# Two conditioning vectors of layer 1 computed on VectorE in layer 0's feed-forward, instead of on TensorE in layer 1's mixer

## The chip, the cores and the metric

The kernel runs on one core of a Trainium2 chip. The metric is device time in microseconds (us) of one execution. Five engines matter here, each with its own queue of instructions that it works off in order: PE (TensorE: matrix products; PEld is its weight load), DVE (VectorE), ACT (ScalarE), POOL (GpSimd, nearly unused) and SP (SyncE, which issues nearly all DMA transfers). An instruction that waits for a semaphore holds back all that stands behind it on its engine.

## The reference

Two blocks of two layers each, on 256 tokens of width 1024, all in float32. The change lies in the first block, whose layers are conditioned by a vector `c`:

```python
c_act = jax.nn.silu(c)
for l in range(DEPTH):                       # DEPTH = 2
    ada = c_act @ w_ada[l] + b_ada[l]        # 1024 x 6144
    sh1, sc1, gt1, sh2, sc2, gt2 = split(ada, 6)
    u = x * (1.0 + sc1) + sh1
    y = mixer(u, ...)                        # projections, attention, 31-tap convolution, gates
    x = layer_norm(DN_ALPHA * x + (1.0 + gt1) * y, ...)
    u = x * (1.0 + sc2) + sh2
    h = square(relu(u @ w_up[l])) @ w_down[l]   # width 4096
    x = layer_norm(DN_ALPHA * x + (1.0 + gt2) * h, ...)
```

Inside the mixer the convolution's output goes through a layer norm over 512 channels (`conformer_conv`) and a SiLU. The second block (three attention branches, gated feed-forward, RMS norms) follows and ends in an RMS norm that is the output, 256x1024.

The six vectors of a layer are numbered 0 to 5 in the order sh1, sc1, gt1, sh2, sc2, gt2; (1, 3) is sh2 of layer 1, (1, 4) is sc2 of layer 1.

## The kernel before, in words

**Weights.** Every weight matrix is cut into pieces of 128x2048 elements (1 MB). `fetch` loads one into `raw` (3 buffers, SP, L133) and splits it into a high part `whi` (ACT CAST, two halves, L139) and the rest `wlo` (DVE subtraction, two halves, L140), 4 buffers each. PE multiplies high by high, high by low and low by high: `ws2` (L176 with `whi`, then L178 with `wlo`) for the feed-forward's up-projection, `as_` (L207, L208, L209, with L208 on `wlo`) for its down-projection, `ws` (L161, L162, L165) elsewhere. So no weight is used before DMA, ACT and DVE are done with it.

**Feed-forward (`ffn1`).** Sixteen pieces of up-weight and sixteen of down-weight, here called u0 to u15 and d0 to d15. A round for column block c does up-weight uc, then the down-weight of three blocks before, d(c-3). Between them ACT squares and DVE splits the activations (L152 writes the low part `s`); the `s4` pool has 7 buffers, so L152 of block c can't write before PE has read the last of the high part of block c-3: it waits for the end of the down-weight d(c-3) on PE. The last three down-weights d13, d14, d15 are held back for the handover, where they are multiplied part by part of the output (`out.tail`). Of these three the first, d13 (`third` in `fetch`), has its high and low part not in `whi` and `wlo` but in the pool `ada`, which has 2 buffers.

**Conditioning.** There are two ways to compute the six vectors.
- On DVE (`ada_work`): per 128x1024 piece one DMA of 512 KB (L397) into the pool `ada`, and one multiply-and-sum instruction (L386, with a short readout behind it) for a vector kept by columns, or L408 and L410 for a gate. Eight pieces make a vector. The load of the next piece is issued before the multiply of the one at hand; with 2 buffers a load waits until the multiply two pieces before is done.
- On PE (`ada_pe`): per quarter of a vector two DMAs of 512 KB (L445), a block of small products (L451, 16 matmul records in the trace), an ACT copy (L454), and products with a column of ones (L461, 4 records, with the sum on DVE in L464) or, for gates, `ada_gate` (L430, L431, L433).

**Side work.** `track` gives a generator a rate, `tick` (called by PE's code with the time of what it has just issued) advances it, `finish` runs out what is left. In layer 0's feed-forward `ada_work` runs 24 pieces (gt2 of layer 0, then sc1 and sh1 of layer 1) with 30 steps per 160 us of ticks; in the mixer of layer 1 `ada_pe` runs three vectors, 12 quarters, with 25 steps per 80 us.

**Order.** PE's order is that of the code. DVE, ACT and SP are ordered by a scheduler when the program is built, except in the handover between two layers (`handover`), which is written out by hand: last parts of the down-projection, gates (L778), residual (L782), statistics (L785 on), normalisation (L795), transposes (L749), and the first products of the next layer.

The functions touched follow, with the profile's line numbers.

Of the kernel before, what the change touches and what calls it, by code (L numbers as in the profile page):

```python
# [12 lines left out]
AF = mybir.ActivationFunctionType  # L13
ALU = mybir.AluOpType
# [46 lines left out]
PARTS = ((0, 512), (512, 768), (768, 1024))  # L61
ADA_PE = [(0, 4), (0, 3), (0, 2), (1, 3), (1, 4), (1, 2)]


class Net:
# [609 lines left out]
    def handover(self, out, ch, nxt=None):  # L675
# [4 lines left out]
        with self.tc.manual_schedule(engines={E.PE, E.DVE, E.Activation}):  # L680
# [3 lines left out]
            fill = ch.front(1)  # L684
# [3 lines left out]
            if ch.ln_rms:  # L688
                out.tail(1, PARTS[2])
            ch.stats(0, itertools.islice(fill, 2))  # L690
            ch.transposed(0, 8 if ch.ln_rms else 0)
# [144 lines left out]
    class RMSNorm(Norm):  # L836
# [66 lines left out]
        def finish(self, h, fill=()):  # L903
            nc, net, u = self.nc, self.net, self.u
            fill = iter(fill)
            if not u:
                y, o = self.y[h], net.out[h * P:(h + 1) * P, :]
                nc.scalar.mul(y[:, :512], y[:, :512], self.rs[h])
                nc.sync.dma_start(o[:, :512], y[:, :512])
                if h:  # L910
                    i = nc.vector.scalar_tensor_tensor(y[:, 512:], net.x[:, h, 512:], self.rs[h], self.g[:, 512:],
                                                       op0=ALU.mult, op1=ALU.mult)
                else:
                    i = nc.vector.tensor_scalar(y[:, 512:], y[:, 512:], self.rs[h], None, op0=ALU.mult)
                nc.sync.dma_start(o[:, 512:], y[:, 512:])
                yield
                yield [i]
                return
# [4 lines left out]
            for k in range(4):  # L923
                i = nc.scalar.copy(hi[k], ps[k])
# [48 lines left out]
    def conv_ln(self, l, cv, hc):  # L973

        nc = self.nc
# [5 lines left out]
        for h in range(2):  # L981
# [6 lines left out]
            z = self.ev()  # L988
            nc.vector.tensor_scalar(z, p, mu, rs, op0=ALU.subtract, op1=ALU.mult)
            zs.append(z)  # L990
# [19 lines left out]
    def mixer1(self, l, u, ps):  # L1010
# [21 lines left out]
        if first:  # L1032
            for ct in range(2):
                self.glu(ps[6 + ct], ct, hp)
            for g in range(3):
                keep(g, ps[2 * g:2 * g + 2] and enumerate(ps[2 * g:2 * g + 2]))
            ada = self.track(self.ada_pe(ADA_PE[:3]), 25, 56)
            conv = self.track(convs[0], 31, 40)
# [5 lines left out]
        else:  # L1044
            keep(2, ps)
            ada = self.track(self.ada_pe(ADA_PE[3:]), 25, 80)
            for ct in range(4):
# [86 lines left out]
    def ffn1(self, l, u, ps):  # L1134
        nc = self.nc
        segs = [(0, 5), (1, 1), (1, 0)] if l == 0 else [(1, 5)]
        ada = self.track(self.ada_work(segs), 8 * len(segs) + 6, 160 if l == 0 else 80)
# [553 lines left out]
```

## Time and profile before

| | |
|---|---|
| median of 3 runs | 1702.15 us (1702.01 to 1704.94) |
| profiled execution | 1700.27 us, of which the trace's span is 1698.5 us |
| mean granted TensorE clock | 0.998 |
| bytes moved by DMA | 347.38 MB, mean 205 GB/s |

The span divides into: start (0 to 65 us), mixer of layer 0 (65 to 195), handover (195 to 222), feed-forward of layer 0 (222 to 395, the last rounds of it from 300), handover (395 to 425, with the last down-weights already from 377), mixer of layer 1 (425 to 570), handover, feed-forward of layer 1 (600 to 770), second block (770 to the end).

In the rows below, times on the left are microseconds from the span's start. In a timeline a row is a run of alike instructions on one engine: start, busy time, engine, line, operation, what is written and read, count, and in brackets how long the engine had been idle before and what released it. A table by windows gives per stretch its length, the busy time of each engine with the number of instructions, the granted clock (1.00 is full), the DMA engines' busy share and GB/s.

### The profile page before, as it was taken

Reading aid. Unit: us, or ns where it says so; the run is one execution under the profiler, and the core shown is the slowest. Engines: PE = TensorE matmul, PEld = TensorE weight load, DVE = VectorE, ACT = ScalarE, POOL = GpSimd, SP = SyncE. Lnnn points to the kernel's source line nnn. Section 1 sums busy time; section 2 is a strip of 40 time slices with the busy share of each in tenths; the row PEclk is TensorE's granted clock in tenths of the full one; section 3 lists DMA queues with packets and bytes.
Section 4 is the critical chain, followed back from the end, with each engine's and each line's share of the span. In section 5 each row is a group of like instructions: output and inputs, shape, how many; then the busy total and the mean of one; then the engine's idle time right before and its main releaser. Section 6 shows DMA issues by size and latency. Waiting matters only on the chain.

```text
span 1698.5 us, 25989 instructions
## 1 busy us (share of the span) xinstructions
PE 1658.0 (98%) x10090; PEld 1437.4 (85%) x10090; DVE 1271.2 (75%) x2485; ACT 955.9 (56%) x1750; POOL 2.6 (0%) x12
## 2 busy tenths in 40 slices
PE   6999999999999999999999999999999999999998
PEld 5888888888888888887988898888889888988887
DVE  7999798588997796568665777766675567877665
ACT  3565375475355475544567755555465687455553
POOL 0000000000000000000000000000000000000000
PEclk9999999999999999999999999999999999999999
DMA  8886468495865386645634443655454444445551
GB/s 343 349 312 232 167 230 340 170 345 209 305 251 201 111 295 216 220 154 194 227 130 152 150 163 138 242 191 198 152 209 170 152 149 149 174 163 209 195 181 46
DMA packets 59975, 347.38 MB, mean 205 GB/s; under 512 B 6558, under 2 KB 10700, under 8 KB 25676
## 3 DMA queue, kind: packets, MB, share of 16 engines
q1 hardware_dynamic: 59852, 345.73, 55.8%
q8 instruction: 79, 1.29, 0.3%
q14 instruction: 44, 0.36, 0.1%
HBM read 344.63 MB, written 2.64 MB: 204 GB/s over the span
## 4 chain that ended last, share of the span: by engine, by line
PE 92%; DVE 5%; ACT 1%; DMA 1%; issue 1%; SPq 0%; DVEq 0%; ACTq 0%
PE ps L176 23%; PE ps L178 12%; PE ps L208 8%; PE ps L209 8%; PE ps L207 8%; PE ps L161 5%; PE ps L162 4%; PE ps L165 4%; PE ps L223 3%; PE ps L229 3%; PE ps L224 3%; PE ps L339 1%; PE ps L451 1%; PE ps L499 1%; PE ps L476 1%; DVE wlo L140 1%
## 5 line engine op out<-in xcount | busy, mean ns | idle before, releaser
L140 DVE TENSOR_TENSOR wlo<-raw,whi 128x1024 fp32r<-128x1024 f32 (+1 forms) x526 | 622.3, 1211 | 242.2 <-ACT whi L139 241.6
L139 ACT CAST whi<-raw 128x1024 fp32r<-128x1024 f32 (+1 forms) x526 | 527.4, 1043 | 266.0 <-PE ps L209 62.3
L176 PE MATMUL ps<-ub,whi 128*128 128x512 f32 x1088 | 273.2, 393 | 0.0
L176 PEld LDWEIGHTS ps<-ub,whi 128*128 128x128 f32 x1088 | 198.6, 188 | 37.5
L207 PE MATMUL ps<-whi,s 128*128 128x512 f32 (+1 forms) x448 | 168.3, 376 | 0.0
L208 PE MATMUL ps<-wlo,s 128*128 128x512 f32 (+1 forms) x448 | 168.1, 375 | 0.0
L209 PE MATMUL ps<-whi,s 128*128 128x512 f32 (+1 forms) x448 | 167.7, 374 | 0.0
L176 PE MATMUL ps<-ua,whi 128*128 128x512 f32 x640 | 165.7, 401 | 0.0
L178 PEld LDWEIGHTS ps<-ub,wlo 128*128 128x128 f32 x1088 | 148.3, 190 | 12.3 <-DVE wlo L140 1.8
L178 PE MATMUL ps<-ub,wlo 128*128 128x256 f32 x1088 | 151.8, 282 | 1.3 <-DVE wlo L140 1.3
L176 PEld LDWEIGHTS ps<-ua,whi 128*128 128x128 f32 x640 | 115.3, 188 | 27.8 <-issue 5.7
L209 PEld LDWEIGHTS ps<-whi,s 128*128 128x128 f32 x448 | 84.3, 188 | 15.9 <-DVE s L152 0.7
L207 PEld LDWEIGHTS ps<-whi,s 128*128 128x128 f32 x448 | 84.5, 189 | 14.5 <-issue 0.6
L189 ACT COPY ev<-ps 128x256 f32<-128x256 f32 x136 | 50.3, 370 | 82.6 <-PE ps L178 82.5
L969 DVE SCALAR_TENSOR_TENSOR s<-s,dw,s 128x255 f32<-128x255 f32 (+14 forms) x240 | 96.7, 461 | 0.0
L208 PEld LDWEIGHTS ps<-wlo,s 128*128 128x128 f32 x448 | 84.5, 189 | 13.6
L178 PEld LDWEIGHTS ps<-ua,wlo 128*128 128x128 f32 x640 | 87.2, 190 | 6.5
L161 PE MATMUL ps<-ua,whi 128*128 128x256 f32 x352 | 89.3, 292 | 0.2 <-DVE s L958 0.2
L178 PE MATMUL ps<-ua,wlo 128*128 128x256 f32 x640 | 89.0, 282 | 0.0
L162 PE MATMUL ps<-ua,whi 128*128 128x256 f32 x352 | 85.9, 282 | 0.0
L161 PE MATMUL ps<-s,whi 128*128 128x256 f32 x320 | 81.9, 288 | 1.3 <-ACT s L151 1.3
L162 PE MATMUL ps<-s,whi 128*128 128x256 f32 x320 | 81.3, 286 | 1.2 <-DVE s L152 1.2
(301 smaller groups left out, 2828.5 us busy)
## 6 DMA issues: line engine op xcount, KB each, us to landing
raw<-in_w_fgu_dram SPq DMA_DIRECT2D x44, 1024.0 KB, 4.8
raw<-in_w_up_dram SPq DMA_DIRECT2D x32, 1024.0 KB, 5.1
raw<-in_w_down_dram SPq DMA_DIRECT2D x32, 1024.0 KB, 5.4
raw<-in_w_in_dram SPq DMA_DIRECT2D x32, 1024.0 KB, 4.8
ada<-in_w_ada_p_dram SPq DMA_DIRECT2D x48, 512.0 KB, 4.4
raw<-in_w_gate_dram SPq DMA_DIRECT2D x24, 1024.0 KB, 4.8
raw<-in_w_fd_dram SPq DMA_DIRECT2D x22, 1024.0 KB, 4.8
raw<-in_w_in_b_dram SPq DMA_DIRECT2D x18, 1024.0 KB, 6.5
```

Source lines behind the costliest of these rows:

```text
L139: nc.scalar.copy(hi[:, a:b], raw[:, a:b])
L140: nc.vector.tensor_sub(lo[:, a:b], raw[:, a:b], hi[:, a:b].bitcast(F32))
L161: mm(ps, whi[:, b], ahi[:, k, :], start=j == 0, stop=False)
L162: mm(ps, whi[:, b], alo[:, k, :], start=False, stop=False)
L165: mm(ps, wlo[:, b], ahi[:, k, :], start=False, stop=j == n - 1)
L176: mm(p2, whi[:, (blk + k) * P:(blk + k + 1) * P], both[:, :, k, :], start=k == 0, stop=False)
L178: mm(p[:, :S], wlo[:, (blk + k) * P:(blk + k + 1) * P], uhi[:, k, :], start=False, stop=k == KT - 1)
L207: mm(ps, ahi[:, k, tok], whi[:, cols], start=first, stop=False, **grp)
L208: mm(ps, ahi[:, k, tok], wlo[:, cols], start=False, stop=False, **grp)
L209: mm(ps, alo[:, k, tok], whi[:, cols], start=False, stop=last, **grp)
L223: mm(p, ahi[:, k, tok], whi[:, cols], start=k == 0, stop=False)
L969: nc.vector.scalar_tensor_tensor(cv[:, ct, d:], hp[:, ct, :S - d], wk, cv[:, ct, d:], op0=ALU.mult, op1=ALU.add)
```

## The change

`ADA_PE` loses (1, 3) and (1, 4): they are computed by `ada_work` in layer 0's feed-forward, which now has 40 pieces instead of 24, with 46 steps per 160 us of ticks instead of 30. The mixer of layer 1 keeps one vector on PE, 4 quarters. Three smaller edits: the convolution's layer norm forms its normalised values on ACT instead of DVE; layer 0's mixer spreads its PE conditioning over 46 us of ticks instead of 56; and the last handover's output is scaled and stored in quarters for the second half of the tokens.

```diff
-ADA_PE = [(0, 4), (0, 3), (0, 2), (1, 3), (1, 4), (1, 2)]
+ADA_PE = [(0, 4), (0, 3), (0, 2), (1, 2)]
@@ handover
-            ch.stats(0, itertools.islice(fill, 2))
+            ch.stats(0, itertools.islice(fill, 2 if ch.u else 3))
@@ RMSNorm.finish, the output
-                nc.scalar.mul(y[:, :512], y[:, :512], self.rs[h])
-                nc.sync.dma_start(o[:, :512], y[:, :512])
+                step = 256 if h else 512
+                for a in range(0, 512, step):
+                    s, r = slice(a, a + step), slice(512 + a, 512 + a + step)
+                    nc.scalar.mul(y[:, s], y[:, s], self.rs[h])
+                    nc.sync.dma_start(o[:, s], y[:, s])
...
@@ conv_ln
-            nc.vector.tensor_scalar(z, p, mu, rs, op0=ALU.subtract, op1=ALU.mult)
+            nm = self.small(1, "nmu")
+            nc.vector.tensor_scalar(nm, mu, -1.0, rs, op0=ALU.mult, op1=ALU.mult)
+            nc.scalar.activation(z, p, AF.Identity, bias=nm, scale=rs)
@@ mixer1, layer 0, then layer 1
-            ada = self.track(self.ada_pe(ADA_PE[:3]), 25, 56)
+            ada = self.track(self.ada_pe(ADA_PE[:3]), 25, 46)
-            ada = self.track(self.ada_pe(ADA_PE[3:]), 25, 80)
+            ada = self.track(self.ada_pe(ADA_PE[3:]), 9, 60)
@@ ffn1
-        segs = [(0, 5), (1, 1), (1, 0)] if l == 0 else [(1, 5)]
+        segs = [(0, 5), (1, 3), (1, 4), (1, 1), (1, 0)] if l == 0 else [(1, 5)]
```

The scheduler puts DVE's and SP's instructions of layer 0's feed-forward in another order. Three places follow. Names end in numbers that count buffers; they differ between the two programs.

**First place: DVE, the L152 from which on conditioning multiplies stand between the weights again, after two rounds without.** Before, this is L152 of block 11 (`s_516`), which waits for the end of d8 on PE; behind it come u12 (`wlo_3270`) and, with one multiply between, d9 (`wlo_3331`).

```order
L152 TENSOR_TENSOR s_516_3325<-ev_3275,s_515_3324 128x512
L431 TENSOR_TENSOR G_495_3193<-ps_3360,b_445_2882 128x256
L433 TENSOR_SCALAR G_495_3193<-G_495_3193 128x256
L386 ISA ada_3264,ada_513_3299<-ada_3264,c_row_92,par_95 128x1024
L386 ISA ada_513_3299 128x1
L140 TENSOR_TENSOR wlo_3270<-raw_3267,whi_3269 128x1024 x2
```

Now it is L152 of block 10 (`s_514`), which waits for the end of d7; behind it come u11 (`wlo_3216`) and then d8 (`wlo_3272`).

```order
L152 TENSOR_TENSOR s_514_3266<-ev_3221,s_513_3265 128x512
L386 ISA ada_3116,ada_478_3039<-ada_3116,c_row_92,par_4_101 128x1024
L386 ISA ada_478_3039 128x1
L386 ISA ada_3145,ada_478_3039<-ada_3145,c_row_92,par_4_101 128x1024
L386 ISA ada_478_3039 128x1
L140 TENSOR_TENSOR wlo_3216<-raw_3213,whi_3215 128x1024
L386 ISA ada_3207,ada_478_3039<-ada_3207,c_row_92,par_4_101 128x1024
L386 ISA ada_478_3039 128x1
L140 TENSOR_TENSOR wlo_3216<-raw_3213,whi_3215 128x1024
L386 ISA ada_3210,ada_478_3039<-ada_3210,c_row_92,par_4_101 128x1024
```

The place lies one round earlier. From it to the end of the feed-forward 21 pieces of conditioning are left on DVE, where before 8 were, and three of them stand ahead of the second half of the first weight behind it, where before there was one.

**Second place: SP, the loads around the first place.** Before, a load of a conditioning piece and a load of a weight alternate; `ada_3364` is the first that waits for a multiply behind L152 of block 11, and `raw_3328` (d9) is ahead of it.

```order
L397 DMA ada_3264<-in_w_ada_t_dram 128x1024
L133 DMA raw_3267<-in_w_up_dram 128x2048
L397 DMA ada_3297<-in_w_ada_t_dram 128x1024
L133 DMA raw_3328<-in_w_down_dram 128x2048
L397 DMA ada_3364<-in_w_ada_t_dram 128x1024
L133 DMA raw_3367<-in_w_up_dram 128x2048
```

Now two conditioning loads stand between two weights; `ada_3207` waits for the multiply of `ada_3116`, and `ada_3210` for that of `ada_3145`.

```order
L397 DMA ada_3116<-in_w_ada_t_dram 128x1024
L397 DMA ada_3145<-in_w_ada_t_dram 128x1024
L133 DMA raw_3213<-in_w_up_dram 128x2048
L397 DMA ada_3207<-in_w_ada_t_dram 128x1024
L397 DMA ada_3210<-in_w_ada_t_dram 128x1024
L133 DMA raw_3269<-in_w_down_dram 128x2048
```

Ahead of the load that waits there is now one weight (u11); d8 (`raw_3269`) stands behind two waiting loads. Before, two weights (u12 and d9) were ahead of it.

**Third place: DVE, the end of layer 0's feed-forward.** Before, the low parts of d13 (`ada_3641`), d14 (`wlo_3694`) and d15 (`wlo_3726`) stand ahead of L152 of block 15 (`s_567`), which waits for the end of d12 on PE; the first two weights of the next layer (`wlo_3734`, `wlo_3742`) stand ahead of L778.

```order
L140 TENSOR_TENSOR ada_3641<-raw_3638,ada_3640 128x1024 x2
L190 TENSOR_TENSOR ev_3646<-ps_3647,ev_3646 128x256
L140 TENSOR_TENSOR wlo_3694<-raw_3691,whi_3693 128x1024 x2
L190 TENSOR_TENSOR ev_3646<-ps_3666,ev_3646 128x256
L140 TENSOR_TENSOR wlo_3726<-raw_3723,whi_3725 128x1024 x2
L152 TENSOR_TENSOR s_567_3688<-ev_3646,s_566_3687 128x512
L140 TENSOR_TENSOR wlo_3734<-raw_3731,whi_3733 128x1024 x2
L140 TENSOR_TENSOR wlo_3742<-raw_3739,whi_3741 128x1024 x2
L778 TENSOR_TENSOR ev_3814<-ps_2560,G_495_3193 128x512
```

Now the low parts of d14 (`wlo_3748`), d13 (`ada_3695`) and d15 (`wlo_3780`) stand behind L152 of block 15 (`s_587`), with two multiplies among them.

```order
L152 TENSOR_TENSOR s_587_3742<-ev_3700,s_586_3741 128x512
L386 ISA ada_3685,ada_562_3586<-ada_3685,c_row_92,par_95 128x1024
L386 ISA ada_562_3586 128x1
L140 TENSOR_TENSOR wlo_3748<-raw_3745,whi_3747 128x1024
L386 ISA ada_3688,ada_562_3586<-ada_3688,c_row_92,par_95 128x1024
L386 ISA ada_562_3586 128x1
L140 TENSOR_TENSOR wlo_3748<-raw_3745,whi_3747 128x1024
L140 TENSOR_TENSOR ada_3695<-raw_3692,ada_3694 128x1024 x2
L140 TENSOR_TENSOR wlo_3780<-raw_3777,whi_3779 128x1024 x2
L767 TENSOR_TENSOR pl_b_3807<-pl_b_3807,ada_562_3586 128x8
L778 TENSOR_TENSOR ev_3868<-ps_2567,G_466_2992 128x512
L140 TENSOR_TENSOR wlo_3788<-raw_3785,whi_3787 128x1024 x2
```

The next layer's two weights (`wlo_3788`, and `wlo_3796` further on) have moved behind L778, one on each side of L782, ahead of the statistics L785. On ACT the casts of d13 (`ada_3694`, which waits for the multiply of `ada_3685`, since it takes that buffer) stand ahead of those of d14 (`whi_3747`).

## Rows read from the trace of the kernel before

**Rows 1.** The page: the chain that ended last, share of the span by engine

```profile
PE 92%; DVE 5%; ACT 1%; DMA 1%; issue 1%; SPq 0%; DVEq 0%; ACTq 0%
```

**Rows 2.** Windows: layer 1's mixer; busy time of PE, PEld, DVE, ACT, POOL

```profile
425.00:500.00 75.00, 75.00 (x597) 63.50 (x599) 71.56 (x166) 34.94 (x64) 0.00 (x0) 1.00 0.75 284
```

**Rows 3.** Window 417 to 486, PE and PEld, instructions of L451 alone

```profile
417.00:486.00 69.00, 8.56 (x128) 3.34 (x128) 1.00 0.83 309
```

**Rows 4.** The same window, instructions of L461 alone

```profile
417.00:486.00 69.00, 4.00 (x32) 4.52 (x32) 1.00 0.83 309
```

**Rows 5.** Timeline of DVE in layer 0's feed-forward, around L152 of block 11

```profile
331.18 0.69 DVE L152 TENSOR_TENSOR s<-ev,s 128x512 fp32r<-128x512 f32 x1 [4.47 <-PE ps L208]
...
332.45 1.28 DVE L386 CUSTOM_DVE_ANT_0 ada<-ada,c_row,par 128x1024 f32<-128x1024 f32 x1
...
333.65 2.35 DVE L140 TENSOR_TENSOR wlo<-raw,whi 128x1024 fp32r<-128x1024 f32 x2
```

**Rows 6.** Timeline of SP's DMA issues: the first one after 305.02

```profile
333.76 0.33 SPq L397 DMA_DIRECT2D ada<-in_w_ada_t_dram  x1
```

**Rows 7.** Windows of 5 us in the same stretch

```profile
325.00:330.00 5.00, 5.00 (x27) 4.25 (x26) 0.42 (x1) 3.56 (x6) 0.00 (x0) 1.00 0.00 0
335.00:340.00 5.00, 5.00 (x30) 4.42 (x31) 5.00 (x6) 0.97 (x3) 0.00 (x0) 1.00 1.00 382
```

**Rows 8.** Timeline of PE: u12 from 331.39, and the first of d9

```profile
331.39 2.19 PE L176 MATMUL ps<-ub,whi 128*128 128x512 f32 x8
334.93 1.21 PE L178 MATMUL ps<-ub,wlo 128*128 128x256 f32 x8 [1.34 <-DVE wlo L140]
...
338.77 0.40 PE L207 MATMUL ps<-whi,s 128*128 128x512 f32 x1
```

**Rows 9.** The page: the largest cast on ACT, and DMA issues with KB and us to landing

```profile
L139 ACT CAST whi<-raw 128x1024 fp32r<-128x1024 f32 (+1 forms) x526 | 527.4, 1043 | 266.0 <-PE ps L209 62.3
...
raw<-in_w_fgu_dram SPq DMA_DIRECT2D x44, 1024.0 KB, 4.8
...
raw<-in_w_in_b_dram SPq DMA_DIRECT2D x18, 1024.0 KB, 6.5
```

**Rows 10.** Timeline of DVE at the end of layer 0's feed-forward

```profile
368.10 2.35 DVE L140 TENSOR_TENSOR ada<-raw,ada 128x1024 fp32r<-128x1024 f32 x2
...
377.37 0.69 DVE L152 TENSOR_TENSOR s<-ev,s 128x512 fp32r<-128x512 f32 x1 [0.64 <-PE ps L208]
377.98 4.62 DVE L140 TENSOR_TENSOR wlo<-raw,whi 128x1024 fp32r<-128x1024 f32 x4
382.52 0.68 DVE L778 TENSOR_TENSOR ev<-ps,G 128x512 f32<-128x512 f32 x1
...
386.02 0.42 DVE L778 TENSOR_TENSOR ev<-ps,G 128x256 f32<-128x256 f32 x1 [1.30 <-PE ps L209]
...
390.57 0.54 DVE L795 TENSOR_SCALAR x<-x,mv,r_r 128x512 f32<-128x512 f32 x1
```

**Rows 11.** Timeline of PE there: d13 begins, its first part of the output ends, the transposes

```profile
377.34 0.40 PE L207 MATMUL ps<-ada,s 128*128 128x512 f32 x1
...
381.29 0.39 PE L209 MATMUL ps<-whi,s 128*128 128x512 f32 x1
...
391.40 1.03 PE L749 MATMUL ps<-con,x 128*128 128x128 f32 x8
```

**Rows 12.** Windows in layer 0's mixer

```profile
160.00:171.00 11.00, 7.87 (x62) 7.28 (x60) 10.88 (x20) 9.86 (x17) 0.00 (x0) 1.00 0.69 255
...
172.00:173.00 1.00, 1.00 (x4) 1.00 (x5) 1.00 (x2) 0.00 (x0) 0.00 (x0) 0.50 0.02 8
...
174.00:175.00 1.00, 1.00 (x7) 1.00 (x6) 1.00 (x2) 0.00 (x0) 0.00 (x0) 0.50 0.89 197
```

**Rows 13.** Timeline of DVE in layer 1's mixer: the convolution's layer norm

```profile
527.00 0.70 DVE L986 BATCH_NORM_STATS2 bn<-ps 128x6 f32<-128x512 f32 x1 [1.61 <-PE ps L984]
...
530.75 0.80 DVE L989 TENSOR_SCALAR ev<-ps,mv,r_r 128x512 f32<-128x512 f32 x1
```

More of the change, by code (lines that the diff above doesn't have):

```diff
@@ L907, in finish @@
                 y, o = self.y[h], net.out[h * P:(h + 1) * P, :]
-                nc.scalar.mul(y[:, :512], y[:, :512], self.rs[h])
-                nc.sync.dma_start(o[:, :512], y[:, :512])
[L910 to L915, printed above, removed]
+                step = 256 if h else 512
[3 more added lines that the diff above has]
+                    nc.sync.dma_start(o[:, s], y[:, s])
+                    if h:
+                        i = nc.vector.scalar_tensor_tensor(y[:, r], net.x[:, h, r], self.rs[h], self.g[:, r],
+                                                           op0=ALU.mult, op1=ALU.mult)
+                    else:
+                        i = nc.vector.tensor_scalar(y[:, r], y[:, r], self.rs[h], None, op0=ALU.mult)
+                    nc.sync.dma_start(o[:, r], y[:, r])
                 yield
```

## The prediction

> **What bounds the kernel now.** I read the chain of waits first: PE holds 92% of it, DVE 5% [rows 1]. So a microsecond less of PE work counts nearly in full wherever PE has no gap, and a microsecond of waiting on DVE counts where PE runs out of weights. Next the windows, because the change takes work from one stage and adds it to another. In layer 1's mixer PE is busy in all 75 us and DVE in 71.56 of them [rows 2]: PE bounds, DVE is close behind. In layer 0's feed-forward the timeline of DVE shows a hole: L152 of block 11 waits 4.47 us for PE, and only behind it come the conditioning multiplies again [rows 5]. SP, whose next conditioning load waits for such a multiply, issues nothing until 333.76 [rows 6], so the DMA engines move nothing at 325 to 330 and then run flat out, 382 GB/s at 335 to 340 [rows 7]. PE pays 1.34 us for it, at the low part of u12 [rows 8]. What the reader is to see: one DVE instruction that waits for the end of a product also stops the loads of the weights two products later.
>
> **What the change takes away.** Eight quarters go from PE in layer 1's mixer, each 16 records of L451 and 4 of L461. In the window 417 to 486 exactly eight ran: 128 records in 8.56 us and 32 in 4.00 [rows 3, 4], together 12.56 us. Records of neighbours overlap a little at their modelled ends, so I take 12.3 (11.5 to 12.56). PE has no gap there, so this is on the path as long as DVE keeps up. DVE loses almost nothing in that stage, and its idle time is 3.4 us of 75 [rows 2], and 1.6 before the convolution's statistics [rows 13]. PE comes to the convolution's transposes 12.3 us sooner; if DVE can only close these 5.0 us, 7.3 are lost again. The other end is no loss, since idle DVE time past 500 helps too and PE has other products to do between the transposes and the use of the normalised values. I take 1.5 lost, near the lower end.
>
> **What it adds: the hole.** Sixteen more multiplies of 1.20 us (start to next start, 332.45 to 333.65 [rows 5]) and sixteen more loads enter layer 0's feed-forward, and the order shows the hole one round earlier, with 21 multiplies left behind it, where 8 were, and one weight loaded ahead of the waiting load, not two. From T, the release of L152 of block 10: L152 0.69, two multiplies 2.40, half a subtraction 1.14 (four take 4.54, 377.98 to 382.52 [rows 10]) give the low part of u11 at T + 4.2. PE wants it 2.2 us after its start, as 1.34 before 334.93 [rows 8], so it stands some 1.9. Then d8: its load is behind a conditioning load that waits for the second multiply, so it is issued at about T + 3.5, with two 0.52 MB loads ahead, the first of them from T + 1.9. 2.1 MB at 382 GB/s take 5.5 us, and a 1 MB load needs 4.8 to land [rows 9], 2.05 more than its bytes; so it lands at T + 9.45. Cast of a half 1.04 [rows 9] and subtraction 1.14: T + 11.6. PE comes from u11 (7.38 with its 1.34 of waiting, so 6.04 [rows 8], and 1.9 here) at T + 8.1 to 9, so it stands 2.6 to 3.3. With half a microsecond on d8's second half that makes 5.2. It isn't won back: a round is 11.15 us (four rounds from 331.39 to 377.34 less 1.34 [rows 8, 11]), and half a round now needs two conditioning loads and a weight, 2.1 MB or 376 GB/s, as much as the queue gave. DVE has 19 multiplies and 20 halves before L152 of block 15, 45.5 us of the 55.8, without the rest of its work. So small waits may follow, up to 2.5. I take 6.5 less the 1.34 that goes: **+5.2** (from +0.5, if only u11 waits, to +6.4).
>
> The Trainium skill ("Perfetto Trace Analysis", Roofline) gives about 435 GB/s as the ceiling of one core's 16 DMA engines. By that 2.1 MB would take 4.8 us and d8 wait 0.7 less; the trace's 382 decides, and nothing above uses the page.
>
> **What it adds: the end of the feed-forward.** Here I am surest. Before, d13's low part is made at 368.10, nine microseconds before L152 of block 15 [rows 10], and PE goes from d12 into d13 without a gap at 377.34 [rows 11]. Now it stands behind that L152, which can't begin before d12 has ended. From E, the end of d12: L152 0.65; the multiply to 1.85, which alone frees the buffer for d13's high part; three casts on ACT at 1.04 (two halves of d13, one of d14) to 4.95; half of d14 on DVE to 6.1; the second multiply to 7.3; d14's second half to 8.4; d13's first half at 9.5. PE's second product of d13 wants it at 0.2, so PE stands **9.3 us**. Without the casts the DVE work alone is 6.4: that is the lower bound.
>
> The handover adds more. The next layer's two weights were subtracted before L778 (four halves from 377.98 [rows 10]); now they sit around L782. The first needs d13's raw buffer, free at E + 10.7: landing after 4.8 at 15.5, cast 16.5, two halves to 18.8; L782 to 19.5; the second weight lands 2.75 later and is done at 21.8; two statistics 0.75; and from the next L778 to L795 it was 4.55 (386.02 to 390.57 [rows 10]), so L795 stands at E + 27.1. Before it stood at 13.2 (377.37 to 390.57). PE's transposes L749 came right behind it [rows 11]. So **+13.9** up to there, PE's 9.3 included. With 6.5 for the load (the median of that weight [rows 9]) it is 15.6; the lower bound stays 6.4.
>
> **What it adds: the clock.** In layer 0's mixer PE was busy only 7.87 of 11 us and then the granted clock fell to 0.50, which is 1.2 instead of 2.4 GHz, in the windows from 172 to 175 [rows 12]: three microseconds that did the work of 1.5. Stands of 9.3 and some 4 us are longer than that. I take **+1.5** (0 to 3.0, for neither or both).
>
> The Trainium skill ("TensorE: Matmul & The Clock Gate", HAM oscillation) says that each long enough idle gap of PE is paid again with a cold start of the next products. By that it would be 3.0; in this trace one drop stands behind two short gaps and the long gap of before isn't there to tell, so I stay at one.
>
> **The small edits.** In layer 0's mixer two DVE instructions go to ACT (the like one takes 0.80 [rows 13]) while PE waits: of 3.1 us idle [rows 12] some may go, but ACT was busy 9.86 of 11 us too. I take -0.6 (-3.1, all of it, to +1.6, the two on ACT late). The output in quarters: no row shows such a store; one 128x512 DVE step of 0.68 [rows 10] is my bound on both sides, 0 my value.
>
> **The sum.** -12.3 + 1.5 + 5.2 + 13.9 + 1.5 - 0.6 = +9.2 us. On the profiled execution's 1700.27 that is 1709.5; the median of the runs is 1.9 higher, so 1711.4. The likeliest case's own range is 1705 to 1718. All low ends together give -9.5 (1692.7), all high ends +23.1 (1725).
>
> **Rivals.**
> - *The cover holds (faster).* The loads catch up, the hole costs 0.5, the end only the 6.4 of DVE's order, and PE's 12.3 shows. Point that decides: whether the two terms in layer 0 together stay below 8 us. 1702.15 + 0.5 + 6.4 - 12.3 - 0.6 = 1696. For it: before, a hole of 28 us in the loads cost only 1.34. Against: d13's place behind L152 doesn't depend on loads. With less at the end than its DVE order says, 1692. Chance 0.17.
> - *About even.* Hole 2, end 9.3, no drop of the clock, nothing given back in the mixer: 1702. Chance 0.08.
> - *The saving isn't one.* DVE sets the mixer's end: 7.3 of the 12.3 are lost there, the rest as forecast: 1702.15 + 9.2 + 5.8 = 1717. For it: DVE at 71.56 of 75 [rows 2]. Against: PE waits for it nowhere in those 75 us. Chance 0.15.
>
> That leaves 0.60 for the forecast. Faster by over 0.2% (3.4 us, about what a measurement here can tell from none) 0.17, within 0.08, slower 0.75. The range goes from 1697, which leaves out about one in ten below, to 1719.
>
> **What would show it.** Right: in the changed profile PE waits 8 to 10 us for the cast or the subtraction of an `ada` tile at the first products behind d12; L749 behind it waits for L795; two or three gaps of 1 to 3 us at L178 and L208 one round ahead of where the 1.34 was; L451 in layer 1's mixer down to four blocks and that stage 10 to 12 us shorter; a stretch at clock 0.50 behind the long gap. Wrong: d13 follows d12 without a gap, or the mixer of layer 1 is as long as before because L984 or the products behind it wait for DVE.

## The result, and the profile after

The changed kernel takes 1726.65 us (median of 5 runs, 1724.21 to 1729.98), the kernel before 1702.15 in the same comparison: ratio 1.0141, 95% interval [1.0126, 1.0155]. It is slower, as forecast, but by 24.5 us where 9.2 were forecast, and outside the stated range, which ended at 1719; even all the high ends of the forecast's terms together gave 1725, so a term was missing and not only mis-sized. The profiled execution has a span of 1724.8 us, 26.3 more than before.

The chain that ended last, of the page after, to be held beside [rows 1]:

```profile
PE 82%; DVE 10%; DMA 4%; ACT 2%; issue 1%; SPq 0%; ACTq 0%; DVEq 0%
```

PE has lost ten hundredths of the chain to DVE, DMA and ACT: it stands where it didn't. To see where, take one mark per stage. The transposes L749 of the second half of the tokens are the last act of each handover that waits. In the timeline of PE, of the kernel before (start, busy time, and in brackets the wait):

```profile
214.16 1.07 PE L749 MATMUL ps<-con,x 128*128 128x128 f32 x8 [1.27 <-DVE x L795]
401.17 1.06 PE L749 MATMUL ps<-con,x 128*128 128x128 f32 x8 [1.27 <-DVE x L795]
587.23 1.07 PE L749 MATMUL ps<-con,x 128*128 128x128 f32 x8 [1.28 <-DVE x L795]
```

and of the kernel after:

```profile
225.57 1.07 PE L749 MATMUL ps<-con,x 128*128 128x128 f32 x8 [1.23 <-DVE x L795]
439.20 1.07 PE L749 MATMUL ps<-con,x 128*128 128x128 f32 x8 [1.28 <-DVE x L795]
612.83 1.07 PE L749 MATMUL ps<-con,x 128*128 128x128 f32 x8 [1.28 <-DVE x L795]
```

The differences between neighbours are the stages' lengths; with the first L161 of layer 0's mixer as the first mark (63.34 before, 65.06 after) and the span's end as the last:

| us | start | layer 0's mixer | its feed-forward | layer 1's mixer | all behind |
|---|---|---|---|---|---|
| before | 63.3 | 150.8 | 187.0 | 186.1 | 1111.3 |
| after | 65.1 | 160.5 | 213.6 | 173.6 | 1112.0 |
| difference | +1.7 | +9.7 | +26.6 | -12.4 | +0.7 |
| forecast | 0 | -0.6 | +20.6 | -10.8 | 0 |

Layer 1's mixer gave more than forecast, the feed-forward cost 6 more, and layer 0's mixer, for which next to nothing was forecast, cost 9.7. The first column varies by up to 2.5 us between the profiled executions of all kernels below, and the second block, which is most of the last, by up to 2.4, whatever was edited, so nothing is read from them. Layer 0's mixer takes 149.6 to 152.5 us wherever its code is as before, so its column is good to about 1.5 us.

**The hole**, timeline of DVE after, to be held beside [rows 5]; the L152 is that of block 10:

```profile
333.51 0.69 DVE L152 TENSOR_TENSOR s<-ev,s 128x512 fp32r<-128x512 f32 x1 [4.47 <-PE ps L208]
...
336.53 1.22 DVE L140 TENSOR_TENSOR wlo<-raw,whi 128x1024 fp32r<-128x1024 f32 x1
339.22 1.28 DVE L386 CUSTOM_DVE_ANT_0 ada<-ada,c_row,par 128x1024 f32<-128x1024 f32 x1 [1.47 <-DMA ada<-in_w_ada_t_dram]
...
340.43 1.22 DVE L140 TENSOR_TENSOR wlo<-raw,whi 128x1024 fp32r<-128x1024 f32 x1
```

SP issues d8 at 337.02, and ACT can cast it only at 344.88 (timelines of SP and ACT, and the window between, in which the DMA engines moved 264 GB/s):

```profile
337.02 0.42 SPq L133 DMA_DIRECT2D raw<-in_w_down_dram  x1
...
344.88 1.99 ACT L139 CAST whi<-raw 128x1024 fp32r<-128x1024 f32 x2 [5.44 <-DMA raw<-in_w_down_dram]
```

```profile
335.00:345.00 10.00, 4.73 (x27) 3.42 (x25) 6.81 (x11) 0.49 (x2) 0.00 (x0) 1.00 0.82 264
```

PE, to be held beside [rows 8]:

```profile
337.81 1.22 PE L178 MATMUL ps<-ub,wlo 128*128 128x256 f32 x8 [2.35 <-DVE wlo L140]
...
341.70 1.21 PE L178 MATMUL ps<-ub,wlo 128*128 128x256 f32 x8 [0.83 <-DVE wlo L140]
345.98 0.49 PE L207 MATMUL ps<-whi,s 128*128 128x512 f32 x1 [3.06 <-ACT whi L139]
347.24 0.80 PE L208 MATMUL ps<-wlo,s 128*128 128x512 f32 x1 [0.77 <-DVE wlo L140]
```

Where PE stood once for 1.34 us it stands four times, 7.0 us in all. The second stand is a new one: a conditioning multiply stands between the two halves of one weight on DVE and waits 1.47 us for its own load, so the weight's second half waits with it.

**The end of the feed-forward**, timeline of PE after, to be held beside [rows 11]: the last product of d12, then d13, then the transposes.

```profile
402.10 0.39 PE L209 MATMUL ps<-whi,s 128*128 128x512 f32 x1
405.38 0.79 PE L207 MATMUL ps<-ada,s 128*128 128x512 f32 x1 [2.90 <-ACT ada L139]
412.01 0.79 PE L208 MATMUL ps<-ada,s 128*128 128x512 f32 x1 [5.83 <-DVE ada L140]
...
429.39 1.07 PE L749 MATMUL ps<-con,x 128*128 128x128 f32 x8 [1.78 <-DVE x L795]
```

and DVE there, to be held beside [rows 10]:

```profile
402.36 0.69 DVE L152 TENSOR_TENSOR s<-ev,s 128x512 fp32r<-128x512 f32 x1 [1.48 <-issue]
402.96 1.28 DVE L386 CUSTOM_DVE_ANT_0 ada<-ada,c_row,par 128x1024 f32<-128x1024 f32 x1
...
407.26 1.23 DVE L140 TENSOR_TENSOR wlo<-raw,whi 128x1024 fp32r<-128x1024 f32 x1 [3.00 <-ACT whi L139]
...
410.74 2.35 DVE L140 TENSOR_TENSOR ada<-raw,ada 128x1024 fp32r<-128x1024 f32 x2
...
428.71 0.54 DVE L795 TENSOR_SCALAR x<-x,mv,r_r 128x512 f32<-128x512 f32 x1
```

The order decided this to within a microsecond: from L152's start at 402.36 the second product of d13 comes 9.65 later and L795 26.35 later, where 9.5 and 27.1 were forecast and 0.2 and 13.2 were before.

**Layer 0's mixer**, timeline of PE after; its stands at L451 of more than half a microsecond, where before there was none:

```profile
76.58 0.64 PE L451 MATMUL ps<-ada,c_sel 128*32 128x256 f32 x8 [0.54 <-DMA ada<-in_w_ada_p_dram]
108.92 0.64 PE L451 MATMUL ps<-ada,c_sel 128*32 128x256 f32 x8 [1.14 <-DMA ada<-in_w_ada_p_dram]
110.43 0.64 PE L451 MATMUL ps<-ada,c_sel 128*32 128x256 f32 x8 [0.87 <-DMA ada<-in_w_ada_p_dram]
125.89 0.64 PE L451 MATMUL ps<-ada,c_sel 128*32 128x256 f32 x8 [1.62 <-DVE s L972]
127.05 0.64 PE L451 MATMUL ps<-ada,c_sel 128*32 128x256 f32 x8 [0.52 <-DMA ada<-in_w_ada_p_dram]
145.59 2.23 PE L451 MATMUL ps<-ada,c_sel 128*32 128x256 f32 x16 [2.07 <-DMA ada<-in_w_ada_p_dram]
```

and behind the convolution:

```profile
175.45 0.66 PE L339 MATMUL ps<-con,ev 128*128 128x128 f32 x4 [2.67 <-ACT ev L994]
```

The first six are the conditioning's own products, and what they wait for is, but for one, a transfer. They belong to the edit from 56 to 46 us of ticks, not to the move: e1, which has that edit alone, has such waits too, and of e3 and e4, which don't have it, e3 has one of 0.50 us and e4 none.

**The clock**, windows after (PE, PEld, DVE, ACT, POOL, granted clock, DMA share, GB/s), to be held beside [rows 12]:

```profile
345.00:350.00 5.00, 3.26 (x8) 2.35 (x9) 4.04 (x5) 2.14 (x3) 0.00 (x0) 0.71 0.80 315
405.00:410.00 5.00, 0.79 (x1) 0.29 (x1) 2.74 (x4) 4.67 (x6) 0.00 (x0) 0.51 1.01 407
410.00:415.00 5.00, 2.99 (x7) 2.37 (x8) 5.00 (x5) 0.49 (x1) 0.00 (x0) 0.50 0.73 260
```

The clock fell to its lower level behind the hole and again in the long stand at d13; there somewhat more than half of the low stretch was idle time. It fell twice in layer 0's mixer too, behind the stands of 2.07 and 2.67 us, where before it fell once [rows 12].

### The profile page after: what moved, and what is told of

It is laid out like the page before. It is cut to its first block, busy times and chain, and to the rows that moved or that the text cites. A ratio compares the mean times of both kernels' runs of the same rounds, so it can differ in the third digit from the quotient of the medians.

```text
span 1724.8 us, 25691 instructions
## 1 busy us (share of the span) xinstructions
PE 1656.0 (96%) x9930; PEld 1433.6 (83%) x9930; DVE 1287.0 (75%) x2510; ACT 956.2 (55%) x1747; POOL 2.6 (0%) x12
## 4 chain that ended last, share of the span: by engine, by line
PE 82%; DVE 10%; DMA 4%; ACT 2%; issue 1%; SPq 0%; ACTq 0%; DVEq 0%
PE ps L176 22%; PE ps L178 11%; PE ps L208 7%; PE ps L209 7%; PE ps L207 7%; PE ps L161 4%; PE ps L162 4%; PE ps L165 3%; PE ps L223 3%; PE ps L229 3%; PE ps L224 3%; DVE wlo L140 3%; DVE s L972 2%; DMA raw<-in_w_down_dram 1%; PE ps L339 1%; ACT whi L139 1%
## 5 line engine op out<-in xcount | busy, mean ns | idle before, releaser
L208 PE MATMUL ps<-wlo,s 128*128 128x512 f32 (+1 forms) x448 | 169.8, 379 | 2.8 <-DVE wlo L140 2.8
L161 PE MATMUL ps<-ua,whi 128*128 128x256 f32 x352 | 89.0, 291 | 0.2 <-DVE s L961 0.2
L207 PE MATMUL ps<-whi,ua 128*128 128x512 f32 (+1 forms) x192 | 69.6, 363 | 13.1 <-ACT ua L151 11.7
L162 PE MATMUL ps<-s,whi 128*128 128x256 f32 x320 | 81.1, 285 | 0.6 <-DVE s L152 0.6
```

The costliest lines, as they stand in the source:

```text
L161: mm(ps, whi[:, b], ahi[:, k, :], start=j == 0, stop=False)
L162: mm(ps, whi[:, b], alo[:, k, :], start=False, stop=False)
L207: mm(ps, ahi[:, k, tok], whi[:, cols], start=first, stop=False, **grp)
L208: mm(ps, ahi[:, k, tok], wlo[:, cols], start=False, stop=False, **grp)
```

## The experiments

Stage lengths are read as above. The kernel before has a median of 1701.55 to 1703.18 in each of the comparisons. The theories named in the first expectations: "turnaround" (two conditioning tiles can't be refilled as fast as the denser steps ask) against "ACT late" for layer 0's mixer; "order" (where DVE's and SP's instructions stand) against "volume" (sixteen loads and multiplies cost the same wherever they stand) for the feed-forward.

**One part alone: the denser steps.**

```diff
-            ada = self.track(self.ada_pe(ADA_PE[:3]), 25, 56)
+            ada = self.track(self.ada_pe(ADA_PE[:3]), 25, 46)
```

> The kernel before with one number changed: layer 0's mixer runs its conditioning on PE with 25 steps per 46 us instead of 56. Theory (turnaround): two conditioning tiles are the whole pool, a quarter's loads can start only when PE has used the last quarter's, and they take 4 to 7 us to land; quarters 5 us apart instead of 7.4 leave no room, so PE waits at L451 for the DMA: 4 to 7 us of L451 waits and 6 to 9 us more in all, 1708 to 1711. Rival (the normalisation on ACT is what made the mixer of layer 0 longer): within 1 us of 1702.

1716.49 us, ratio 1.0077 [1.0062, 1.0092]: +13.3, more than any theory said. Layer 0's mixer is 164.3 long (150.8 before), all other stages as before. This one number costs as much as the whole move. L451 waits 4.3 us for DMA in sum and 2.3 for DVE; the window of 100 to 150, where PE was busy 49.05 us in the kernel before, reads

```profile
100.00:150.00 50.00, 43.44 (x386) 34.46 (x385) 49.96 (x143) 27.16 (x68) 0.00 (x0) 0.97 0.77 285
```

Behind the convolution L339 stands 2.55 us, and at 175 to 200 the mean granted clock is 0.82. All stands of PE in this stage up to the handover add up to 13.5 us, where they were 5.4 before; and by windows of 1 us the granted clock is at 0.50, its lower level, for 13.7 us, where it was for 3.4. Half of these 10.2 us more, 5.1, is an estimate of what the clock cost; with the 8.1 of stands that makes 13.2 of the stage's 13.5.

**One part alone: the normalisation on ACT.** The `conv_ln` part of the diff, on the kernel before.

> The kernel before with the convolution's normalised values formed on ACT instead of DVE, nothing else. Theory (turnaround): 1701 to 1704, since the stand at L430 behind which it lies only changes its name. Rival (ACT late): L339 waits 2.7 us for ACT and the clock falls behind it: 1705 to 1707.

1702.58 us, ratio 1.0002 [0.9992, 1.0011]: nothing. "ACT late" falls; L339 waits for ACT in the changed kernel because the conditioning that PE did there before is used up. In e1, with the normalisation on DVE, it waits as long, for DVE.

**One part alone: the move.** `ADA_PE`, `segs` and the track of layer 1's mixer, on the kernel before.

> The move of the two vectors alone, with layer 0's mixer, the convolution's norm and the output as before. Theory: layer 0's feed-forward and handover lose 26 us (as measured with all edits), layer 1's mixer wins 12.4: 1714 to 1718. Rival (half of the 26 comes from what the mixer of layer 0 hands on: its later weights and order): 1704 to 1710.

1716.63 us, ratio 1.0080 [1.0065, 1.0095]: +13.5. Feed-forward 213.7, layer 1's mixer 173.6: as in the changed kernel. So the two stages' change doesn't come from what was done to layer 0's mixer.

**The changed kernel without the denser steps.**

> The changed kernel with 25 steps per 56 us in layer 0's mixer as before. Theory (turnaround): the L451 waits of 5.5 us for DMA go and with them 6 to 9 us: 1717 to 1720, L451 without waits. Rival (ACT late): 1724 to 1727, with L339 still waiting 2.7 us for ACT.

1719.12 us, ratio to the kernel before 1.0094 [1.0077, 1.0111]; layer 0's mixer 151.8, no wait at L451. 7.5 us less than the changed kernel. That is less than e1's 13.3; the traces fit that the stretch behind the convolution suffers less with the normalisation on ACT (mean clock 0.93 at 175 to 200 in the changed kernel, 0.82 in e1), but no run tells this apart. So the 24.5 us are 13.5 of the move (e3), 7.5 of the denser steps, 2.5 by which e4 lies above e3 (the normalisation and the last handover), and 1.0 by which the kernel before differs between the two comparisons.

**The end of the feed-forward mended.** In e3:

```diff
-        ada = self.track(self.ada_work(segs), 8 * len(segs) + 6, 160 if l == 0 else 80)
+        ada = self.track(self.ada_work(segs), 8 * len(segs) + 6, 110 if l == 0 else 80)
```

> The move of the two vectors alone (as measured: 1716.6), with its steps denser, 46 per 110 us of ticks instead of 160, so that the conditioning ends a round and a half earlier and d13, d14 and d15 stand ahead of L152 of block 15 on DVE as in the kernel before; the hole at block 10 is still there. Theory (order): from the end of d12 to the transposes L749 14 to 16 us instead of 27, no stand of PE at d13: 1703 to 1706. Rival (volume: sixteen more loads and multiplies cost the 26 us wherever they stand): 1713 or more.

1706.89 us, ratio 1.0028 [1.0016, 1.0041]. d13 begins at 395.19 without a gap and L749 comes 14.75 later, as before the change (14.06); in the changed kernel it comes 27.29 after d12's last product, which is 0.23 ahead of where d13 could begin. The end is some 12.3 us shorter with the same sixteen pieces, so it wasn't their number that cost there but where they stood. The stage, 202.8, is 10.9 shorter than in e3, and the median 0.9 above what was expected, because the hole got deeper with the denser steps: one cast is waited for 4.92 us there.

**The hole mended.** In e3, the bias table's preparation moves to layer 1's feed-forward:

```diff
-        rel = self.track(self.rel_bias(), 5, 60) if l == 0 else None
+        rel = self.track(self.rel_bias(), 5, 60) if l == 1 else None
```

> The move alone, with the preparation of the second block's bias table (L606 to L625: small loads, two products, a store and a load through DRAM) in layer 1's feed-forward instead of layer 0's. In the order of DVE the two rounds without conditioning multiplies are gone then, and d13's subtraction stands ahead of L152 of block 15. Theory (order): DMA busy share never 0 in layer 0's feed-forward, no stand over 1 us on PE there, mixer of layer 1 still 12.4 shorter: 1689 to 1695. Rival (volume): 1708 or more.

1700.25 us, ratio 0.9984 [0.9975, 0.9994]. The hole is gone: from the handover on PE has no stand until

```profile
380.01 0.80 PE L207 MATMUL ps<-ada,s 128*128 128x512 f32 x1 [2.75 <-ACT ada L139]
...
384.89 0.80 PE L208 MATMUL ps<-ada,s 128*128 128x512 f32 x1 [4.09 <-DVE ada L140]
```

So the two rounds without multiplies came from the bias table's small store and load, round which the scheduler ordered the rest. The expectation (1689 to 1695) was missed by 5, and on the end: in the order d13's subtraction stood ahead of L152, but two multiplies that free d13's buffer still stood late, and 6.8 us of stand stayed. The feed-forward is 195.6; 1.8 us went to layer 1's with the table.

One thing here bears on all that follows. Up to d13, PE loses nothing to the sixteen pieces (windows of this run):

```profile
222.00:300.00 78.00, 78.00 (x401) 66.47 (x400) 72.01 (x91) 50.67 (x73) 0.00 (x0) 1.00 0.82 302
300.00:370.00 70.00, 70.00 (x359) 59.80 (x358) 59.18 (x87) 37.31 (x54) 0.00 (x0) 1.00 0.85 311
```

From the handover's first L749 to the end of d12 it takes 169.9 us, and 169.8 in the kernel without the sixteen pieces whose table stands in the same place (e11 below), although all loads of the forty pieces but the last had been issued by 373. Nearly all of the 11.7 us by which this stage is longer than e11's lie at d13 and behind it.

**The turnaround.** In e1, the two loads of a quarter go side by side into one 8 KB tile of the same pool, and the next quarter's loads are issued one quarter ahead, so that the pool holds two quarters, in twice the room:

```diff
-                    w = self.t("ada", [P, 4, 256])
-                    nc.sync.dma_start(w, i["w_ada_p"][j, n, kh])
+            w = self.t("ada", [P, 2, 4, 256])
+            for kh in range(2):
+                nc.sync.dma_start(w[:, kh], i["w_ada_p"][j, n, kh])
...
+                ws = nxt
+                if n < 3 or (l, seg) != segs[-1]:
+                    nxt = load(*((j, n + 1) if n < 3 else (ADA_PE.index(segs[segs.index((l, seg)) + 1]), 0)))
```

> The kernel before with 25 steps per 46 us in layer 0's mixer (as measured: 1716.5), and the two loads of a quarter of PE's conditioning put side by side in one tile of the same pool, so that the next quarter's loads are issued one quarter ahead. Theory (turnaround): L451 waits for DMA below 0.5 us in sum where it was 4.3, 1707 to 1712; what is left above 1702 is the stand at L339, behind which PE has no conditioning left to do. Rival (DMA rate or DVE's load sets it): 1715 or more.

1714.30 us, ratio 1.0074 [1.0057, 1.0090], between the two theories, so it decides for neither. L451 waits for no transfer any more, and the window 100 to 150 is as full as before:

```profile
100.00:150.00 50.00, 49.02 (x460) 41.35 (x462) 48.86 (x140) 29.97 (x72) 0.00 (x0) 1.00 0.83 306
```

But the loads issued ahead brought a stand of their own (L466 and L459 are L461 and L454 of the kernel before):

```profile
90.02 1.01 PE L466 MATMUL ps<-ones,ev 128*128 128x1 f32 x4 [7.00 <-ACT ev L459]
```

ACT was 6.95 us behind, waiting for a weight that SP had issued only at 77.47, after a conditioning load whose tile wasn't free. The turnaround theory is right for the waits at L451; that the mixer gets its time back is not shown, and in this form it doesn't (160.7).

**The changed kernel with both mended in part.** e4 with the bias table moved.

> The changed kernel with 25 steps per 56 us in layer 0's mixer as before, and the bias table's preparation in layer 1's feed-forward. Theory (order and turnaround): as the move with the bias table moved, the normalisation on ACT and the output in quarters adding within 2 us either way: 1688 to 1695. Rival (volume): 1708 or more.

1704.24 us, ratio 1.0007 [0.9998, 1.0016]: 9 us above the expectation. Feed-forward 198.3, with stands of 2.96 and 5.20 at d13 and 2.05 at the gates; against the kernel before nothing is won.

**Hole and end both mended.** e6 with 130 instead of 160 us of ticks (e9), and with 120 (e10). In the order d13 is behind no multiply.

> The move alone, with the bias table's preparation in layer 1's feed-forward (no hole) and 46 steps per 130 us of ticks, so that on DVE the last conditioning multiply stands a round ahead of L152 of block 15 and d13 behind none of them. Theory (order): layer 0's feed-forward and handover within 3 us of the kernel before, of which 1.7 go to layer 1's feed-forward with the table; layer 1's mixer 12.4 shorter: 1690 to 1694. Rival (volume): some 8 us stay, as with the bias table moved alone (1700): 1698 or more.

1701.20 us, ratio 1.0001 [0.9991, 1.0010].

> As e9, with 46 steps per 120 us. Theory (order): the same 1690 to 1694, since the order at the end of the feed-forward is the same. Rival (volume: denser loads and multiplies cost more): 2 us or more above e9.

1699.96 us, ratio 0.9987 [0.9975, 0.9998]. Both miss 1690 to 1694. They don't test "order" alone: to get d13 clear of the multiplies they also make the steps denser, 0.35 and 0.38 per us of ticks where e6 has 0.29. In e9 d13 begins 179.6 us after the handover's first L749, 9.9 later than in e11, and L749 comes 15.1 behind it, 1.1 later; e6 lost about the same sum at the other end. Layer 1's mixer is 173.6 in both, but the feed-forward still takes 194.8 and 196.2. In e9 there is one stand at the gates and two at weights, with the granted clock at 0.50 for some three microseconds behind the first at a weight:

```profile
279.83 2.08 PE L176 MATMUL ps<-ub,whi 128*128 128x512 f32 x8 [2.63 <-DVE G L431]
...
341.79 0.50 PE L208 MATMUL ps<-wlo,s 128*128 128x512 f32 x1 [2.42 <-DVE wlo L140]
...
368.13 0.50 PE L208 MATMUL ps<-wlo,s 128*128 128x512 f32 x1 [1.94 <-DVE wlo L140]
```

**Controls.** The kernel before with the bias table moved, and with the two edits of the last handover:

> The kernel before with nothing changed but the place of the bias table's preparation (layer 1's feed-forward). Theory: its hole goes too, and with it the 1.34 us at L178 and no more: 1700 to 1702.5. Rival (the gain of the kernels with the table moved comes from the table, not from the move of the vectors): 1694 or less.

1701.16 us, ratio 0.9997 [0.9988, 1.0006]. The table's place alone wins nothing in all: the feed-forward of layer 0 falls to 183.8, that of layer 1 grows by 1.8.

> The kernel before with the last handover's two edits alone (output in quarters, one fill step more). Theory: within 0.7 us of the kernel before, either way. Rival (they cost the 2 us by which the end of the changed kernels is longer): 1704 to 1706.

1703.60 us, ratio 1.0008 [0.9999, 1.0016]: +2.05 by the medians, +1.4 by the ratio. That is over the 0.7 of the theory and just under the rival's 1704, and the interval holds both nothing and 2.7 us, so it stays open. In the profiled execution layer 0's feed-forward, where nothing was edited, is 1.3 us longer.

**Loads or multiplies.** e9 with the sixteen loads left out, and e9 with the sixteen multiplies cut to 8 of 1024 columns:

```diff
+            same = n + 1 < len(items) and items[n + 1][:2] in ((1, 3), (1, 4))
-            w, nxt = nxt, load(*items[n + 1]) if n + 1 < len(items) else None
+            w, nxt = nxt, (nxt if same else load(*items[n + 1])) if n + 1 < len(items) else None
```

> As e9 (1701.2), but the sixteen pieces added to layer 0's feed-forward aren't loaded: their multiplies run on a tile that is already there, so the two vectors of layer 1 come out wrong. Theory (the loads, put in SP's one queue among the weights, cost the 8 to 11 us that are left in layer 0's feed-forward): from the first L749 before it to the first behind it 186 us or less, where e9 has 194.8, and 1690 to 1694. Rival (DVE's multiplies cost them): 192 or more there and 1698 to 1702.

```diff
-        self.nc.vector.tensor_tensor_reduce(w, w, self.c_row, 0.5, b[:, k:k + 1], ALU.mult, ALU.add,
+        self.nc.vector.tensor_tensor_reduce(w, w, self.c_row[:, :w.shape[-1]], 0.5, b[:, k:k + 1], ALU.mult, ALU.add,
...
-                self.ada_dot(l, seg, k, w)
+                self.ada_dot(l, seg, k, w[:, :8] if (l, seg) in ((1, 3), (1, 4)) else w)
```

> As e9, with all loads, but the sixteen added multiplies work on 8 of 1024 columns, so the two vectors come out wrong. Theory (loads): 192 or more from L749 to L749 and 1698 to 1702. Rival (DVE's multiplies): 186 or less there and 1690 to 1694.

1690.28 us, ratio 0.9922 [0.9907, 0.9937], and 1696.44, ratio 0.9971 [0.9959, 0.9983]. Feed-forward 185.1 and 190.95. The first is as the theory had it; the second lies between the theory (192 or more) and the rival (186 or less), so most of the cost goes with the loads, not all. Measured from the 183.8 of e11, which has the table in the same place and none of the sixteen pieces: multiplies alone +1.3, loads with short multiplies +7.1, both together (e9) +11.0. The 2.6 by which both together exceed the sum is as large as the stand at the gates (2.63), which neither e13 nor e14 has. The windows 300 to 390, first e9, then without loads, then with short multiplies:

```profile
300.00:390.00 90.00, 85.42 (x424) 71.47 (x423) 72.92 (x102) 50.11 (x71) 0.00 (x0) 0.98 0.87 309
```

```profile
300.00:390.00 90.00, 90.00 (x467) 77.18 (x466) 77.94 (x110) 49.96 (x70) 0.00 (x0) 1.00 0.84 305
```

```profile
300.00:390.00 90.00, 83.76 (x432) 70.89 (x431) 70.81 (x103) 49.00 (x68) 0.00 (x0) 1.00 0.88 319
```

DVE with 77.94 of 90 us busy doesn't hold PE up; with the loads in the queue PE stands, although the DMA engines are busy no more than 0.88 on the mean. Leaving the loads out also changes the scheduler's order, which these two runs don't hold fixed. And the loads cost this at e9's density: e6 has the same sixteen, and up to d13 they cost nothing that can be seen.

**One vector instead of two.** e9 with (1, 4) back on PE, so 32 pieces, 38 steps per 140 us, which is 0.27 per us; layer 1's mixer runs its two vectors with 17 steps per 70 us. In SP's order two conditioning loads stand between two weights at 12 of 20 places and one at the others; in e9 it is two at all 20, in the kernel before at 3 of 21. So the place wasn't mended to "one, as before".

```diff
-ADA_PE = [(0, 4), (0, 3), (0, 2), (1, 2)]
+ADA_PE = [(0, 4), (0, 3), (0, 2), (1, 4), (1, 2)]
-        segs = [(0, 5), (1, 3), (1, 4), (1, 1), (1, 0)] if l == 0 else [(1, 5)]
+        segs = [(0, 5), (1, 3), (1, 1), (1, 0)] if l == 0 else [(1, 5)]
```

> The version that the experiments point to: only (1, 3) moves (32 pieces, 38 steps per 140 us), (1, 4) and (1, 2) stay on PE, the bias table in layer 1's feed-forward. In the order one conditioning load then stands between two weights, as before, and d13 stands two rounds ahead. Theory (two loads between two weights are what the queue can't carry): half the saving, 6.2, at 1 to 3 us of cost in the feed-forward: 1695 to 1699. Rival (each piece costs the same 0.6 us): 1700 to 1702.

1695.55 us, ratio 0.9954 [0.9941, 0.9966]: faster than the kernel before and than the changed one. The feed-forward is 184.1, 0.3 above e11, and layer 1's mixer 180.1, 6.0 less. Eight pieces cost nothing that can be seen, sixteen cost 11, so each piece doesn't cost the same. But their density changed too: 0.27 steps per us here and 0.29 in e6 up to d13 cost nothing, 0.35 in e9 cost 9.9. What eight pieces allow is to end ahead of d13 at the lower density. The theory that two loads between two weights can't be carried isn't borne out, since 12 such places stand here. PE in the feed-forward has no stand at all between the handovers.

## Why the prediction was wrong

The sign and the two mechanisms in the feed-forward were right; the size was not, and the step that failed first is **"the small edits"**, which left out a change of its own, the denser steps. The second is the size of **the hole**. Without the small edits the forecast would have been +9.8, and the move alone measured +13.5 (e3): off in size, but inside the range.

- **"I take -0.6" for layer 0's mixer.** The term weighed the two DVE instructions that went to ACT and gave the 46 for 56 us no price at all. Measured alone, the normalisation is nothing (e2) and the denser steps +13.3 (e1); in the changed kernel the stage is 9.7 longer. A warning could have been read from the trace before. There the blocks of L451 start at 69.28, 76.65 and 84.02, 7.4 us apart; the pool holds one quarter; a load lands 4.4 us after its issue on the median of the whole run and up to 6.5, and is issued when the block before has run. In the changed kernel two blocks start 5.07 apart (83.52 and 88.59) and the median landing is 5.4. What could be read was that there was no room: at 46 for 56 the 7.4 become 6.1 (an estimate), and a quarter's second load goes out 1.1 us after the block before it starts and needs 4.4 more. That it would cost 13.3 no row showed. A step of a generator had been taken as work that is only moved, without asking what its loads wait for.
- **The hole, "+5.2".** The place and the kind of the waits were right (u11, then d8); the size was not. From the start of L152 of block 10 to that of block 15 the feed-forward lost 10.7 us (58.1 before, 68.85 after), over the high end of 6.4. The four stands are 7.0 of it, where the working had 5.2 for them. It left out u11's second half (0.83), and it had d8 land 9.45 us after the release: the load was issued at 3.5, as worked out, but the cast could begin only at 11.4, since the queue gave 264 GB/s there and not 382. Small stands behind them are 2.0, inside the 2.5 that were allowed; the 1.34 goes off. The other 3.0 are no stand: the granted clock fell to 0.50 behind these stands, for some 3.4 us by windows of 1 us, which by estimate is 1.7 of them, about what the forecast had as its term for the clock. The last 1.3 stay open. And 2.8 us were lost ahead of that L152 (from the handover's first L223 to it 111.1 before, 114.0 after), for which nothing was forecast: a stand of 1.23 at the gates, and four of the gates' products that now come ahead of it.
- **The end of the feed-forward, "+13.9", and the clock, "+1.5".** Measured +13.0 (27.0 from the start of L152 of block 15 to L749, where 14.0 were), with a drop of the clock inside it. The second product of d13 came 9.45 us later than before, after a forecast of 9.3. e5 confirms it by taking it away. The 27.1 for L795 were near in part by luck: the next layer's first weight didn't wait for d13's buffer, free at 10.7 in the working, but was issued 8.5 us after that L152 began, when d14 was done, and then waited with its subtraction behind L778, which waited 2.33 us for PE.
- **The saving, "-12.3" and "1.5 lost".** -12.4: nothing was given back, in any kernel with the move. DVE did close up (busy 74.49 of the 75 us from 463 to 538, where 71.56 were), and PE had no stand there, so the rival in which DVE sets the mixer's end was wrong.
- **The output in quarters, 0**: not decided; e12 has +1.4 or +2.05, over the bound of 0.68, but zero lies inside its interval.

Of the clock, a drop was taken once; in the feed-forward there are two, behind the hole (0.71 at 345 to 350) and in the stand at d13 (0.50), and none behind the 1.78 us before L749. The Trainium skill ("TensorE: Matmul & The Clock Gate", HAM oscillation) has each long enough idle gap followed by a cold start; the trace agrees with that for the two long ones (3.06 us in the hole, and 2.90 with 5.83 behind it at d13). It fell behind shorter ones too, 2.07 and 2.67 us in layer 0's mixer.

## What to carry to other kernels

Before a generator's rate is raised, compare the time between two of its steps with the time that its loads need to land, divided by the tiles that its pool can hold ahead: that one number cost 13 us alone here. A transfer put into an in-order issue queue has to be priced by what stands behind it while it waits for its buffer, and not by its bytes alone. And when work moves to an engine with spare time, ask two things of its spacing: whether the queue carries its loads at that density, and whether it ends before the last buffers are wanted. Here sixteen pieces met one of the two at either spacing, and eight met both.

## What the runs showed that had not been expected

The same sixteen pieces cost 11 to 12 us in two quite different places: at 46 steps per 160 us all of it at the end (e6), at 130 nearly all of it ahead of d13 (e9); eight cost none. The mean load of the queue doesn't tell these apart: at 300 to 370 the DMA engines moved 311 GB/s in e6 and in e9, at a busy share of 0.85 and 0.89, and PE stands only in e9. No run gave d13 a buffer outside the pool `ada` at e6's spacing, which would have been the test of whether all sixteen can be had for nothing. A store and load of a small table through DRAM, issued in the middle of the stage, decided through the scheduler's order where the conditioning stood for two rounds of 11 us. That the longer multiplies make the weights wait by freeing tiles later is not what the traces show: the stands at weights are 4.4 us in e9 and 6.3 in e14, whose multiplies are short. In layer 0's mixer in e1 the stands and the clock add up to the loss, but why PE stands so much longer behind the convolution was not tested apart.
